# A hybrid decoder layer: low-part score products in 64-row pairs, attention steps of two heads per key head, x chunks in three pieces

## The chip, the cores and the metric

The kernel runs on one core of one Trainium2 chip. The metric is device microseconds of one execution; the figure given for a kernel is the median of several runs. The profile is of one execution of its own, and its times are counted from the start of its span.

## The reference

One layer over 16 learned meta tokens and 1024 tokens of 1024 features, in float32:

```python
u = rmsnorm(h, g_pre_mix)
q, k, v, xr, yr = split(u @ w_in)       # 512, 128, 128, 512, 512 columns
attn = sliding_window_attention_with_sinks(q, k, v, sinks)   # 8 heads of 64, 2 key heads
xr = causal_depthwise_conv(xr, conv_w, conv_b)               # 4 taps
hr = rg_lru(xr, w_a, b_a, w_x, b_x, lru_lambda)              # gates, then a scan over time
h = h + rmsnorm(concat(attn, gelu(yr) * hr) @ w_out, g_post_mix)
h = h + rmsnorm(square(relu(rmsnorm(h) @ w_ff1)) @ w_ff2, g_post_ffn)
```

In the attention a block of 128 queries sees two blocks of 128 keys, its own and the one before, of which the mask leaves a window of 128. Four query heads share one key head: heads 0 to 3 the first, 4 to 7 the second. Each head has a sink, a score without a value.

## The kernel before

Operands of matmuls have the type float32r. Each is split into a high part (a cast to that type on ACT, L96) and a low part (what the cast leaves over, a subtraction on DVE, L99). A product is then three matmuls into one bank of PSUM: high by high, high by low, low by high (`mm3`, L125, L130, L131). Weights are split in this way as they arrive.

The work on the core runs in stages.

- **Opening stage.** The tokens come in four pieces (`ALL`: 272, 256, 256, 256). Of each piece the rows are normed and transposed into `u`, and projected to keys, to values, to the first query pair (`q0`) and to the first x chunk (`xr0`). The first piece is written out by hand with `part` (L282), the others go through `project`, one bank of 24 matmuls per weight and piece. The columns of `u @ w_in` are handled 128 at a time. A query pair j holds heads j and j + 4, one of each key head. The weights of the first x chunk are loaded (L383) ahead of the last four loads of x (L147).
- **Attention stage.** Eight steps: query pair j = 0 to 3, and half = 0, 1 (four query blocks each). `scores(j, half, q)` makes the scores of both heads of the pair for four blocks and turns them into softmax weights; `attend` of the step before transposes the weights (L675), splits them, masks them with selects on POOL (L680) and multiplies them with the values (L691). Between the two, `next_fill` puts one projection of 128 columns on the list: q1, x1, q2, x2, q3, x3, then the four y chunks (the last two of these between the gates). A fill of q or y goes in two pieces of 512 tokens (`REAL2`), one of x in the four of `ALL`, followed by its convolution on DVE (L715, L720).
- **Gates** of the recurrence (L817): 64-row matmuls, two at a time on the two halves of the rows, in pieces of 348, 348 and 344 tokens; then the scan, the output projection, and the two feed-forward products, which fill the rest of the span.

Queries are stored so that one matmul does two of the three products. `q[h]` has the high part of head h in its own 64 rows and the low part in the other 64. `khh[h]` has the high keys in both halves. One matmul of 128 rows (L625) therefore sums high by high and low by high. The second (L629) multiplies `q[h]` with `kl[h]`, which holds the low keys in the head's own rows and zeros in the others:

```python
nc.tensor.matmul(dst, q[h][:, c], hi, start=True, stop=False)    # L625
nc.tensor.matmul(dst, q[h][:, c], lo, start=False, stop=True)    # L629
```

Each matmul has 256 columns, the keys of two blocks. Two blocks of one head share a bank of the tag `s`, of which there are two; ACT copies the scores of the own block out (L642) and DVE those of the block before that the mask keeps (L643). The first query block takes its keys from `km`, where the meta tokens stand.

What an engine does next is set by a planner: it walks through the instructions of the program in the order of their priority, simulates the times, and gives an engine the first instruction whose operands and buffers are ready. Fills are issued with `deferred`, at a lower priority, so they go where attention work waits. Buffers come from groups with a fixed count (`b` 17, `c` 8, `d` 4, `ws` 5, and two banks each of `acc`, `s`, `pt`, `o`).

Of the kernel before, what the change touches and what calls it, by code (L numbers as in the profile page):

```python
# [37 lines left out]
def hybrid_layer(  # L38
# [30 lines left out]
    def f32(ap):  # L69
        return ap.bitcast(F32)  # L70
# [217 lines left out]
    ALL = [(0, 272), (272, 256), (528, 256), (784, 256)]  # L288
    REAL2 = [(16, 512), (528, 512)]

    khh = [slot("b", [P, T], F32R) for _ in range(2)]
    kl = [slot("b", [P, T], F32R) for _ in range(2)]
    HALF = (slice(0, HD), slice(HD, P))
    for h in range(2):
        nc.gpsimd.memset(f32(kl[h][HALF[1 - h]]), 0.0)

# [99 lines left out]
    load_x(3)  # L398
    rx = fetch([(X_COL, P)], "e")
    for i in range(4, 8):  # L400
# [9 lines left out]
    km = slot("ws", [P, 4, 2 * P], F32R)  # L410
    nc.gpsimd.memset(f32(km[:, 0:2, 0 : P - NMETA]), 0.0)
    nc.gpsimd.memset(f32(km[:, 2:4, :]), 0.0)
    nsink = const.tile([P, 8], F32, name="nsink")
# [21 lines left out]
    def low_k(hh, lo, src):  # L435
        return [
            nc.vector.tensor_tensor(
                lo[h][HALF[h]], src[HALF[h]], f32(hh[h][HALF[h]]), op=ALU.subtract
            ).ins
            for h in range(2)  # L440
        ]

    def sink_k(acc, t0, n):
        o = NMETA if t0 == 0 else 0
        c = slice(t0 + o - NMETA, t0 - NMETA + n)
        parts = [([khh[0][:, c], khh[1][:, c]], [kl[0][:, c], kl[1][:, c]], acc[:, o:])]
        if o:

            m, mk = slice(0, NMETA + P), slice(P - NMETA, 2 * P)
            parts.append(  # L450
                ([km[:, 0, mk], km[:, 1, mk]], [km[:, 2, mk], km[:, 3, mk]], acc[:, m])
            )
        ops = [[], []]
        for hh, lo, src in parts:
            ops[0] += high_k(hh, src)
        for hh, lo, src in parts:
            ops[1] += low_k(hh, lo, src)
        if o:
            for e in range(2):
                for ins in ops[e]:  # L460
                    chained(e, ins)
# [34 lines left out]
    q0, sink_q0 = new_q()  # L496
    xr0, sink_x0 = new_x("c")
    for b in range(4):
# [3 lines left out]
        if b == 0:  # L502
# [10 lines left out]
            sink_v(acc[1][:, : piece[1]], *piece)  # L513
            wx = high_w(rx)
            low_w(wx, rx)
            for w, (t0, n), sink, tag in (
                (wq, (16, 256), sink_q0, "o"), (wx, piece, sink_x0, "acc"),
            ):
# [8 lines left out]
        project(wq, [piece], sink_q0)  # L527
        project(wx, [piece], sink_x0)
        done.append(last_mm[0])
# [78 lines left out]

    def scores(j, half, q):

# [4 lines left out]
        for h in range(2):  # L615
            nc.gpsimd.tensor_copy(
                sn[:, h, :, P], nsink[:, j + 4 * h : j + 4 * h + 1].to_broadcast([P, 4])
            )
        for h in range(2):
            for bp in range(2):  # L620
                sp_ = bank("s", (P, 2, 256))

                def qk(dst, b, hi, lo):
                    c = slice(b * P, (b + 1) * P)
                    nc.tensor.matmul(  # L625
                        dst, q[h][:, c], hi, start=True, stop=False,
                        skip_group_check=True,
                    )
                    nc.tensor.matmul(  # L629
                        dst, q[h][:, c], lo, start=False, stop=True,  # L630
                        skip_group_check=True,
                    )

                for i in range(2):
                    b = 4 * half + 2 * bp + i
                    if b == 0:
                        qk(sp_[:, i, :], b, km[:, h, :], km[:, 2 + h, :])
                    else:
                        c = slice((b - 1) * P, (b + 1) * P)
                        qk(sp_[:, i, :], b, khh[h][:, c], kl[h][:, c])  # L640
                s_ = sn[:, h, 2 * bp : 2 * bp + 2, 0:P]
                nc.scalar.copy(s_, sp_[:, :, P:256])  # L642
# [3 lines left out]
                )  # L646
                if half == 0 and bp == 0:
                    w = slice(0, P - NMETA)
                    nc.vector.copy_predicated(
                        sn[:, h, 0, w], above_i[:, w], far.to_broadcast([P, P - NMETA])  # L650
                    )
            nc.vector.tensor_reduce(
                negm[:, h, :], sn[:, h], axis=mybir.AxisListType.X, op=ALU.min
# [12 lines left out]

    def attend(j, half, sn):
        flat = sn.rearrange("p a b c -> p (a b c)")
        pp = []
        for h in range(2):  # L670
# [7 lines left out]
            for p_ in (ph, pl):  # L678
                for s, g, op in ((1, 1, ALU.is_ge), (0, -1, ALU.is_gt)):
# [3 lines left out]
                    )  # L683
            pp.append([t_.rearrange("p a b c -> p (a b c)") for t_ in (ph, pl)])
        for h in range(2):
            po = bank("o")

            def av(kb, oc, n, pc, first, last):
                v = vm[:, h, :] if kb == 0 else vk[h][:, kb - 1, :]
                for k, p_ in enumerate(pp[h]):  # L690
                    nc.tensor.matmul(  # L691
                        po[:, oc : oc + n], v, p_[:, pc : pc + n],
                        start=first and k == 0, stop=last and k == 1,
                        skip_group_check=True,
                    )

            kb0 = 4 * half
            av(kb0, 0, P, 0, True, False)
            for i in range(3):
                av(kb0 + 1 + i, i * P, 256, P + 256 * i, False, False)  # L700
            av(kb0 + 4, 3 * P, P, 7 * P, False, True)

# [3 lines left out]
            nc.vector.tensor_tensor(whole, po[r, :], whole, op=ALU.add)  # L706
        ah, al = at[half][j // 2]
        split(ah[:, j % 2, :], al[:, j % 2, :], flat[:, 0:512])

# [25 lines left out]
    def fill_x(c):  # L735
        def run(w):
            xr, sink = new_x()
            project(w, ALL, sink)
            conv(c, xr, "b" if c == 3 else "d")
        return run  # L740
# [12 lines left out]

    qs = [q0] + [None] * 3
    conv(0, xr0)
    fills = []
    for kind, j in (("q", 1), ("x", 1), ("q", 2), ("x", 2), ("q", 3), ("x", 3)):
        if kind == "q":
# [15 lines left out]
    prev = None  # L774
    for j in range(NPAIR):
        for half in range(2):
            if j % 2 == 0 and half == 0:
                at_pair(j // 2)
            gate_after = last_lut[0]
            sn = scores(j, half, qs[j])  # L780
            if True:
                with deferred(FILL_LAG):
                    next_fill()
            if prev is not None:
                attend(*prev)
            prev = (j, half, sn)
    attend(*prev)


# [14 lines left out]
    def gates(c):  # L804
# [4 lines left out]
        z = [slot("c", [P, TT]) for _ in range(2)]  # L809
        for t0, n in ((0, 348), (348, 348), (696, 344)):  # L810
            acc = []
# [697 lines left out]
```

## Time and profile before

| | |
|---|---|
| timed runs | 961.83, 956.39, 958.47 us, median 958.47 |
| span of the profiled execution | 955.3 us; the profile gives no other time for it |
| mean granted clock of TensorE | 0.998 |
| opening stage, first score product | to about 60 us |
| attention stage | about 60 to 186 us |
| gates | 196.6 to 211 us |
| matmuls in the whole kernel | 4728 |
| score products | 64 at L625, 64 at L629 |
| attention products | 160 at L691 |

The profile's lines give start and duration of an instruction or a group, the engine, the line of the source, the operation, output and input by the program's names (buffer numbers left out), and for a matmul rows and columns of the weights and of the moving operand. PE is TensorE's matmul side, PEld its loading of weights, DVE VectorE, ACT ScalarE, POOL GpSimd, SP SyncE, whose queue issues most DMAs.

### The profile page before, as it was taken

To read this page: it belongs to the slowest core of one execution; us is meant where nothing else is said; L and a number is where in the kernel's file an instruction comes from. 1 tells how busy PE (TensorE), PEld (TensorE's weight loads), DVE (VectorE), ACT (ScalarE), POOL (GpSimd) and SP (SyncE) were. 2 spreads that over 40 slices of the span, in tenths; PEclk is the share of its full clock that TensorE was granted. 3 is DMA by queue.
4 is the path that set the end of the run, shared out by engine and by line. 5 is a ranking of instruction groups with operands and counts; after the bars stand their busy time and mean duration, and the time that the engine had idled before them with its cause. 6 is when DMAs were issued, how large, how long until landed. Compare 5 with 4: busy or idle time off the path is not lost.

```text
span 955.3 us, 12432 instructions
## 1 busy us (share of the span) xinstructions
PE 943.8 (99%) x4728; PEld 789.7 (83%) x4728; DVE 655.7 (69%) x845; ACT 505.9 (53%) x854; POOL 129.1 (14%) x189
## 2 busy tenths in 40 slices
PE   9999999999999999999999999999999999999996
PEld 8999999877888878888888888888887788888885
DVE  6567987788856787665644465476667576779893
ACT  7537766568645554444655575654433343446441
POOL 4102563520021100010000000001121100001201
PEclk9999999999999999999999999999999999999999
DMA  8221010204226368674422364334777765647934
GB/s 271 56 67 23 24 45 24 67 23 131 83 109 185 133 220 264 198 253 144 155 89 88 111 203 127 104 113 114 175 180 186 185 199 177 192 139 196 246 65 89
DMA packets 88199, 130.21 MB, mean 136 GB/s; under 512 B 13702, under 2 KB 52630, under 8 KB 88140
## 3 DMA queue, kind: packets, MB, share of 16 engines
q1 hardware_dynamic: 78972, 104.44, 34.0%
q0 software_dynamic: 8880, 24.19, 12.2%
q8 instruction: 37, 0.61, 0.3%
q10 hardware_dynamic: 288, 0.79, 0.2%
q14 instruction: 22, 0.18, 0.1%
HBM read 109.93 MB, written 18.87 MB: 135 GB/s over the span
## 4 chain that ended last, share of the span: by engine, by line
PE 88%; DVE 5%; ACT 3%; DMA 2%; POOL 1%; issue 1%; SPq 0%; DVEq 0%; ACTq 0%; POOLq 0%
PE ps_acc L130 10%; PE ps_acc L131 10%; PE ps_acc L125 10%; PE ps_s L131 6%; PE ps_s L130 6%; PE ps_s L125 6%; PE ps_pt L130 6%; PE ps_pt L131 6%; PE ps_pt L125 6%; PE ps_o L130 5%; PE ps_o L131 5%; PE ps_o L125 5%; ACT c L82 1%; PE ps_o L691 1%; PE ps_acc L282 1%
## 5 line engine op out<-in xcount | busy, mean ns | idle before, releaser
L99 DVE TENSOR_TENSOR ws<-raw,ws 128x1024 fp32r<-128x1024 f32 (+1 forms) x69 | 82.6, 1197 | 76.1 <-ACT ws L96 24.3
L96 ACT CAST ws<-raw 128x1024 fp32r<-128x1024 f32 (+1 forms) x68 | 69.7, 1026 | 87.9 <-PE ps_o L130 23.9
L96 ACT CAST ws<-e 128x1024 fp32r<-128x1024 f32 x41 | 43.0, 1049 | 82.8 <-PE ps_o L130 35.3
L125 PE MATMUL ps_acc<-a,ws 128*128 128x256 f32 (+2 forms) x256 | 85.8, 335 | 0.0
L130 PE MATMUL ps_acc<-a,ws 128*128 128x256 f32 (+2 forms) x256 | 85.5, 334 | 0.0
L131 PE MATMUL ps_acc<-a,ws 128*128 128x256 f32 (+2 forms) x256 | 85.0, 333 | 0.0
L99 DVE TENSOR_TENSOR b<-b,b 128x1024 fp32r<-128x1024 f32 (+2 forms) x50 | 58.9, 1177 | 24.8 <-PE ps_o L130 19.1
L96 ACT CAST b<-b 128x1024 fp32r<-128x1024 f32 (+2 forms) x49 | 49.9, 1019 | 46.4 <-DVE b L996 41.0
L99 DVE TENSOR_TENSOR ws<-e,ws 128x1024 fp32r<-128x1024 f32 x41 | 50.1, 1223 | 32.4 <-ACT ws L96 18.9
L680 POOL TENSOR_SCALAR_AFFINE_SELECT c<-c 128x512 fp32r<-128x512 f32 x64 | 53.6, 858 | 67.6 <-ACT c L96 59.3
L125 PEld LDWEIGHTS ps_acc<-a,ws 128*128 128x128 f32 x256 | 48.3, 189 | 4.7 <-issue 0.2
L131 PEld LDWEIGHTS ps_acc<-a,ws 128*128 128x128 f32 x256 | 48.3, 189 | 4.5
L130 PEld LDWEIGHTS ps_acc<-a,ws 128*128 128x128 f32 x256 | 48.2, 188 | 4.4 <-issue 0.4
L125 PE MATMUL ps_acc<-ws,b 128*128 128x512 f32 (+1 forms) x120 | 46.3, 387 | 1.1 <-ACT ws L96 1.1
L130 PE MATMUL ps_acc<-ws,b 128*128 128x512 f32 (+1 forms) x120 | 46.3, 386 | 0.5 <-DVE ws L99 0.4
L131 PE MATMUL ps_acc<-ws,b 128*128 128x512 f32 (+1 forms) x120 | 46.1, 385 | 0.0
L125 PE MATMUL ps_pt<-ws,b 128*128 128x512 f32 x112 | 44.4, 396 | 0.0
L130 PE MATMUL ps_pt<-ws,b 128*128 128x512 f32 x112 | 44.1, 394 | 0.0
L131 PE MATMUL ps_pt<-ws,b 128*128 128x512 f32 x112 | 44.0, 393 | 0.0
L125 PE MATMUL ps_s<-ws,b 128*128 128x512 f32 x110 | 43.4, 395 | 0.0
L131 PE MATMUL ps_s<-ws,b 128*128 128x512 f32 x110 | 43.3, 394 | 0.0
L130 PE MATMUL ps_s<-ws,b 128*128 128x512 f32 x110 | 43.3, 393 | 0.0
(416 smaller groups left out, 2662.0 us busy)
## 6 DMA issues: line engine op xcount, KB each, us to landing
raw<-in_w_ff_dram SPq DMA_DIRECT2D x61, 512.0 KB, 4.1
e<-in_w_ff_dram SPq DMA_DIRECT2D x45, 512.0 KB, 4.0
a<-in_w_ff_dram SPq DMA_DIRECT2D x12, 512.0 KB, 6.6
s_dram<-a POOLq DMA_DIRECT2D x12, 512.0 KB, 3.7
c<-in_x_dram SPq DMA_DIRECT2D x8, 512.0 KB, 4.0
raw<-in_w_in_dram SPq DMA_DIRECT2D x8, 512.0 KB, 3.7
d<-in_x_dram SPq DMA_DIRECT2D x8, 512.0 KB, 3.3
out_dram<-raw SPq DMA_DIRECT2D x8, 512.0 KB
```

Source lines behind the costliest of these rows:

```text
L82: ins = nc.scalar.activation(*args, **kwargs).ins
L96: nc.scalar.copy(hi, src)
L99: low = nc.vector.tensor_tensor(lo, src, f32(hi), op=ALU.subtract).ins
L125: ins = nc.tensor.matmul(dst, lh, rh, start=start, stop=False, skip_group_check=True).ins
L130: nc.tensor.matmul(dst, lh, rl, start=False, stop=False, skip_group_check=True)
L131: last_mm[0] = nc.tensor.matmul(dst, ll, rh, start=False, stop=stop, skip_group_check=True).ins.name
L282: last_mm[0] = nc.tensor.matmul(acc[:, :n], w[k // 2][:, kc, :], u[kc][k % 2][:, t0 : t0 + n], start=k == 0 and kc == 0, stop=k == last an ...
L680: nc.gpsimd.affine_select(out=p_[:, :, s], in_=f32(p_[:, :, 0]), pattern=[[0, 4], [g, P]], compare_op=op, fill=0.0, base=0, channel_multip ...
L691: nc.tensor.matmul(po[:, oc : oc + n], v, p_[:, pc : pc + n], start=first and k == 0, stop=last and k == 1, skip_group_check=True,)
```

## The change

- The low keys of both key heads stand in one tile `kl`, each in its own half. Their products take only the head's own 64 rows, of the queries as of the keys. For each query block the order is now: high product of head 0, of head 1 (128 rows), low product of head 0, of head 1 (64 rows), with a bank for each head.
- A step of the attention has two query pairs (so two heads per key head) and two query blocks (a quarter), in place of one pair and four blocks. In `attend`, one matmul covers both heads of a key head, with an operand and an output of two runs of columns: three matmuls for each part of the weights, where there were five.
- The second query pair (`q1`) is projected in the opening stage, where the first x chunk was; the x chunk becomes the first fill. The fills are then x0, q2, x1, q3, x2, x3, and the y chunks as before.
- The x chunks are projected in three pieces of 348, 348 and 344 tokens (`THIRDS`).

```diff
@@ -287,14 +287,13 @@
     ALL = [(0, 272), (272, 256), (528, 256), (784, 256)]
     REAL2 = [(16, 512), (528, 512)]
+    THIRDS = [(0, 348), (348, 348), (696, 344)]
     khh = [slot("b", [P, T], F32R) for _ in range(2)]
-    kl = [slot("b", [P, T], F32R) for _ in range(2)]
+    kl = slot("b", [P, T], F32R)
     HALF = (slice(0, HD), slice(HD, P))
-    for h in range(2):
-        nc.gpsimd.memset(f32(kl[h][HALF[1 - h]]), 0.0)
     zeros = slot("ws", [P, 512], F32R)
@@ -396,7 +395,7 @@
     load_x(2)
     load_x(3)
-    rx = fetch([(X_COL, P)], "e")
+    rq1 = fetch([(Q_COL + HD, HD), (Q_COL + 5 * HD, HD)], "e")
     for i in range(4, 8):
         load_x(i)
@@ -408,8 +407,7 @@
     low_w(wq, rq)
     km = slot("ws", [P, 4, 2 * P], F32R)
-    nc.gpsimd.memset(f32(km[:, 0:2, 0 : P - NMETA]), 0.0)
-    nc.gpsimd.memset(f32(km[:, 2:4, :]), 0.0)
+    nc.gpsimd.memset(f32(km[:, 0:3, 0 : P - NMETA]), 0.0)
     nsink = const.tile([P, 8], F32, name="nsink")
     nc.sync.dma_start(nsink, attn_sinks[0].partition_broadcast(P))
@@ -435,7 +433,7 @@
         return [
             nc.vector.tensor_tensor(
-                lo[h][HALF[h]], src[HALF[h]], f32(hh[h][HALF[h]]), op=ALU.subtract
+                lo[HALF[h]], src[HALF[h]], f32(hh[h][HALF[h]]), op=ALU.subtract
             ).ins
             for h in range(2)
@@ -443,12 +441,12 @@
         o = NMETA if t0 == 0 else 0
         c = slice(t0 + o - NMETA, t0 - NMETA + n)
-        parts = [([khh[0][:, c], khh[1][:, c]], [kl[0][:, c], kl[1][:, c]], acc[:, o:])]
+        parts = [([khh[0][:, c], khh[1][:, c]], kl[:, c], acc[:, o:])]
         if o:
             m, mk = slice(0, NMETA + P), slice(P - NMETA, 2 * P)
             parts.append(
-                ([km[:, 0, mk], km[:, 1, mk]], [km[:, 2, mk], km[:, 3, mk]], acc[:, m])
+                ([km[:, 0, mk], km[:, 1, mk]], km[:, 2, mk], acc[:, m])
             )
         ops = [[], []]
@@ -494,7 +492,7 @@
     done = [None, None]
     q0, sink_q0 = new_q()
-    xr0, sink_x0 = new_x("c")
+    q1, sink_q1 = new_q()
     for b in range(4):
         if b:
@@ -511,10 +509,10 @@
             part(acc[1], wv, piece, 2)
             sink_v(acc[1][:, : piece[1]], *piece)
-            wx = high_w(rx)
-            low_w(wx, rx)
+            wq1 = high_w(rq1)
+            low_w(wq1, rq1)
             for w, (t0, n), sink, tag in (
-                (wq, (16, 256), sink_q0, "o"), (wx, piece, sink_x0, "acc"),
+                (wq, (16, 256), sink_q0, "o"), (wq1, (16, 256), sink_q1, "acc"),
             ):
                 acc = bank(tag)
@@ -525,7 +523,7 @@
         project(wv, [piece], sink_v)
         project(wq, [piece], sink_q0)
-        project(wx, [piece], sink_x0)
+        project(wq1, [piece], sink_q1)
         done.append(last_mm[0])
     for h in range(2):
@@ -606,49 +604,50 @@
-    def scores(j, half, q):
+    def scores(jp, quarter):
         sn = slot("c", [P, 2, 4, P + 1])
...
         rden = small.tile([P, 2, 4], F32, name="rden", tag="rden")
         for h in range(2):
-            nc.gpsimd.tensor_copy(
-                sn[:, h, :, P], nsink[:, j + 4 * h : j + 4 * h + 1].to_broadcast([P, 4])
-            )
-        for h in range(2):
-            for bp in range(2):
-                sp_ = bank("s", (P, 2, 256))
-
-                def qk(dst, b, hi, lo):
-                    c = slice(b * P, (b + 1) * P)
+            for jj in range(2):
+                k = 2 * jp + jj + 4 * h
+                nc.gpsimd.tensor_copy(
+                    sn[:, h, 2 * jj : 2 * jj + 2, P], nsink[:, k : k + 1].to_broadcast([P, 2])
+                )
+        for jj in range(2):
+            q = qs[2 * jp + jj]
+            sps = [bank("s", (P, 2, 256)) for _ in range(2)]
+            for i in range(2):
+                b = 2 * quarter + i
+                cq, ck = slice(b * P, (b + 1) * P), slice((b - 1) * P, (b + 1) * P)
+                for h in range(2):
                     nc.tensor.matmul(
-                        dst, q[h][:, c], hi, start=True, stop=False,
-                        skip_group_check=True,
+                        sps[h][:, i, :], q[h][:, cq],
+                        khh[h][:, ck] if b else km[:, h, :],
+                        start=True, stop=False, skip_group_check=True,
                     )
+                for h in range(2):
+                    r = HALF[h]
                     nc.tensor.matmul(
-                        dst, q[h][:, c], lo, start=False, stop=True,
-                        skip_group_check=True,
+                        sps[h][:, i, :], q[h][r, cq], kl[r, ck] if b else km[r, 2, :],
+                        start=False, stop=True, skip_group_check=True,
                     )
-
-                for i in range(2):
-                    b = 4 * half + 2 * bp + i
-                    if b == 0:
-                        qk(sp_[:, i, :], b, km[:, h, :], km[:, 2 + h, :])
-                    else:
-                        c = slice((b - 1) * P, (b + 1) * P)
-                        qk(sp_[:, i, :], b, khh[h][:, c], kl[h][:, c])
-                s_ = sn[:, h, 2 * bp : 2 * bp + 2, 0:P]
+            for h in range(2):
+                sp_ = sps[h]
+                s_ = sn[:, h, 2 * jj : 2 * jj + 2, 0:P]
                 nc.scalar.copy(s_, sp_[:, :, P:256])
                 nc.vector.copy_predicated(
...
                     sp_[:, :, 0:P],
                 )
-                if half == 0 and bp == 0:
+                if quarter == 0:
                     w = slice(0, P - NMETA)
                     nc.vector.copy_predicated(
-                        sn[:, h, 0, w], above_i[:, w], far.to_broadcast([P, P - NMETA])
+                        sn[:, h, 2 * jj, w], above_i[:, w], far.to_broadcast([P, P - NMETA])
                     )
+        for h in range(2):
             nc.vector.tensor_reduce(
                 negm[:, h, :], sn[:, h], axis=mybir.AxisListType.X, op=ALU.min
@@ -664,7 +663,7 @@
         return sn
-    def attend(j, half, sn):
+    def attend(jp, quarter, sn):
         flat = sn.rearrange("p a b c -> p (a b c)")
         pp = []
@@ -681,31 +680,32 @@
                         compare_op=op, fill=0.0, base=0, channel_multiplier=-g,
                     )
-            pp.append([t_.rearrange("p a b c -> p (a b c)") for t_ in (ph, pl)])
+            pp.append((ph, pl))
+        kb0 = 2 * quarter
         for h in range(2):
             po = bank("o")
-
-            def av(kb, oc, n, pc, first, last):
-                v = vm[:, h, :] if kb == 0 else vk[h][:, kb - 1, :]
+            two = po.rearrange("p (j c) -> p j c", j=2)
+            for n, (oc, pc, w) in enumerate(((0, 0, P), (0, P, 2 * P), (P, 3 * P, P))):
+                kb = kb0 + n
+                v = vk[h][:, kb - 1, :] if kb else vm[:, h, :]
                 for k, p_ in enumerate(pp[h]):
                     nc.tensor.matmul(
-                        po[:, oc : oc + n], v, p_[:, pc : pc + n],
-                        start=first and k == 0, stop=last and k == 1,
+                        two[:, :, oc : oc + w], v,
+                        p_.rearrange("p (j i) s c -> p j (i s c)", j=2)[:, :, pc : pc + w],
+                        start=n == 0 and k == 0, stop=n == 2 and k == 1,
                         skip_group_check=True,
                     )
-
-            kb0 = 4 * half
-            av(kb0, 0, P, 0, True, False)
-            for i in range(3):
-                av(kb0 + 1 + i, i * P, 256, P + 256 * i, False, False)
-            av(kb0 + 4, 3 * P, P, 7 * P, False, True)
             r, o = HALF[h], HALF[1 - h]
...
             nc.scalar.copy(whole, po[o, :])
             nc.vector.tensor_tensor(whole, po[r, :], whole, op=ALU.add)
-        ah, al = at[half][j // 2]
-        split(ah[:, j % 2, :], al[:, j % 2, :], flat[:, 0:512])
+        ah, al = at[quarter // 2][jp]
+        c = slice(256 * (quarter % 2), 256 * (quarter % 2) + 256)
+        split(
+            ah[:, :, c], al[:, :, c],
+            flat[:, 0:512].rearrange("p (j c) -> p j c", j=2),
+        )
@@ -735,7 +735,7 @@
         def run(w):
             xr, sink = new_x()
-            project(w, ALL, sink)
+            project(w, THIRDS, sink)
             conv(c, xr, "b" if c == 3 else "d")
         return run
@@ -751,10 +751,9 @@
         return run
-    qs = [q0] + [None] * 3
-    conv(0, xr0)
+    qs = [q0, q1, None, None]
     fills = []
-    for kind, j in (("q", 1), ("x", 1), ("q", 2), ("x", 2), ("q", 3), ("x", 3)):
+    for kind, j in (("x", 0), ("q", 2), ("x", 1), ("q", 3), ("x", 2), ("x", 3)):
         if kind == "q":
             fills.append((lambda j=j: w_q(j), fill_q(j)))
@@ -772,18 +771,16 @@
     prev = None
-    for j in range(NPAIR):
-        for half in range(2):
-            if j % 2 == 0 and half == 0:
-                at_pair(j // 2)
+    for jp in range(2):
+        at_pair(jp)
+        for quarter in range(4):
             gate_after = last_lut[0]
-            sn = scores(j, half, qs[j])
-            if True:
-                with deferred(FILL_LAG):
-                    next_fill()
+            sn = scores(jp, quarter)
+            with deferred(FILL_LAG):
+                next_fill()
             if prev is not None:
                 attend(*prev)
-            prev = (j, half, sn)
+            prev = (jp, quarter, sn)
     attend(*prev)
@@ -807,7 +804,7 @@
         z = [slot("c", [P, TT]) for _ in range(2)]
-        for t0, n in ((0, 348), (348, 348), (696, 344)):
+        for t0, n in THIRDS:
             acc = []
             for s in range(2):
```

## The prediction

> **What bounds the kernel now.** I read the page first: busy shares, then the chain that ended last; then the busy time by stretches of 20 us; then the PE timeline of the attention stage, matmul by matmul.
>
> ```profile
> PE 943.8 (99%) x4728; PEld 789.7 (83%) x4728; DVE 655.7 (69%) x845; ACT 505.9 (53%) x854; POOL 129.1 (14%) x189
> ...
> PE 88%; DVE 5%; ACT 3%; DMA 2%; POOL 1%; issue 1%; SPq 0%; DVEq 0%; ACTq 0%; POOLq 0%
> ```
>
> PE is busy for 99% of the 955.3 us and carries 88% of the chain. But busy PE is not PE at its peak, so the stage that the change touches (scores, softmax and attention products, with projections as filling work between them) has to be looked at by itself. The columns are: stretch, its length, then busy time and count of instructions of PE, PEld, DVE, ACT and POOL, the granted clock, DMA share and GB/s.
>
> ```profile
> 20.00:40.00 20.00, 20.00 (x170) 19.64 (x169) 13.77 (x30) 12.06 (x30) 5.11 (x13) 1.00 0.31 81
> ...
> 100.00:120.00 20.00, 20.00 (x134) 18.24 (x133) 19.45 (x31) 13.31 (x42) 12.06 (x13) 1.00 0.09 28
> 120.00:140.00 20.00, 20.00 (x156) 19.21 (x155) 17.54 (x30) 13.77 (x45) 12.25 (x18) 1.00 0.15 43
> 140.00:160.00 20.00, 19.68 (x138) 18.25 (x137) 16.39 (x28) 12.75 (x37) 8.48 (x13) 1.00 0.13 38
> ```
>
> PE has nearly no idle time in the stage, although DVE is close behind it (19.45 of 20). Filling projections cover every softmax. So here the sum of PE's issue intervals sets the end: each interval removed or added on PE moves it by as much, and time saved on ACT, DVE or POOL moves nothing. The duration of a matmul (about 280 ns at 256 columns) is not its price, because matmuls overlap; the price is the step from one start to the next:
>
> ```profile
> 73.99 0.28 PE L625 MATMUL ps_s<-ws,b 128*128 128x256 f32 x1
> ...
> 74.81 0.28 PE L629 MATMUL ps_s<-b,b 128*128 128x256 f32 x1
> ```
>
> These are the first and the last of a group of eight score products: seven intervals take 0.82 us, 0.117 each, which I use for 256 columns.
>
> **The change part by part.** First the low parts of the scores.
>
> ```profile
> L625 PE MATMUL ps_s<-b,b x56: 275/281/366, 65.8 to 165.8; 128*128 128x256 f32 x56
> ...
> L625 PE MATMUL ps_s<-ws,b x8: 278/282/367, 59.7 to 155.1; 128*128 128x256 f32 x8
> ```
> ```profile
> L629 PE MATMUL ps_s<-b,b x56: 275/280/288, 66.0 to 165.9; 128*128 128x256 f32 x56
> ...
> L629 PE MATMUL ps_s<-ws,b x8: 279/281/282, 59.9 to 155.2; 128*128 128x256 f32 x8
> ```
>
> There are 64 high products (L625) and 64 low ones (L629). The high ones stay. The 64 low ones become 64-row products of the two heads, rows 0 to 63 and 64 to 127, in separate banks, so as 32 pairs. The gates (L817) already run such pairs, and show both what a pair costs and what it costs to get in and out of 64-row work:
>
> ```profile
> 196.29 0.40 PE L125 MATMUL ps_acc<-a,ws 128*128 128x512 f32 x1
> 196.62 0.43 PE L817 MATMUL ps_s<-b,e 64*128 64x348 f32 x1
> 196.62 0.43 PE L817 MATMUL ps_pt<-b,e 64*128 64x348 f32 x1
> 196.89 0.32 PE L817 MATMUL ps_o<-b,e 64*128 64x348 f32 x1
> 196.89 0.32 PE L817 MATMUL ps_s<-b,e 64*128 64x348 f32 x1
> ...
> 198.00 0.32 PE L817 MATMUL ps_pt<-b,e 64*128 64x344 f32 x1
> 198.00 0.32 PE L817 MATMUL ps_o<-b,e 64*128 64x344 f32 x1
> 198.25 0.51 PE L130 MATMUL ps_acc<-a,ws 128*128 128x512 f32 x1
> 198.59 0.40 PE L131 MATMUL ps_acc<-a,ws 128*128 128x512 f32 x1
> ...
> 200.21 0.40 PE L125 MATMUL ps_acc<-a,ws 128*128 128x512 f32 x1
> ```
>
> The two of a pair start together, so a pair costs one interval: seven intervals from 196.89 to 198.00, 0.159 each at 348 columns. A 512-column matmul costs 0.231 (seven intervals from 198.59 to 200.21). Pairing therefore saves half the low products: 32 x 0.117 = 3.8 us.
>
> Now the switch. From the start at 196.29 to that at 198.59 are 2.30 us. They hold two 512-column intervals (0.46) and nine pairs (9 x 0.159 = 1.43), 1.89 in all. So 0.41 us are spent on going in and out. The first matmul on either side also shows a longer time (0.43 against 0.32, 0.51 against 0.40), as if it waited until the pipe had emptied: a 512-column matmul that lasts 0.40 and frees its place after 0.231 leaves 0.17 to wait, and the switch is 0.2 each way. The next gate block repeats it to the hundredth, which a wait for data would not:
>
> ```profile
> 201.59 0.40 PE L125 MATMUL ps_acc<-a,ws 128*128 128x512 f32 x1
> ...
> 203.89 0.40 PE L131 MATMUL ps_acc<-a,ws 128*128 128x512 f32 x1
> ```
>
> The new loop issues, for each query block: high, high, low pair. So it goes into 64-row work and out again 32 times (2 key steps x 4 quarters x 2 heads x 2 blocks): 32 x 0.41 = 13.1 us. A 256-column matmul leaves the same to wait as a 512-column one (0.28 - 0.117 = 0.16), so I see no reason for less. What the gates don't show is a short run. The nearest row is the transposes of 8 rows between transposes of 128:
>
> ```profile
> 22.15 0.38 PE L357 MATMUL ps_pt<-ident,d 128*128 128x128 f32 x2
> 22.37 0.38 PE L357 MATMUL ps_s<-ident,d 128*128 128x128 f32 x2
> ```
> ```profile
> 52.60 0.38 PE L357 MATMUL ps_s<-ident,d 128*128 128x128 f32 x2
> 52.91 0.41 PE L539 MATMUL ps_o<-ident,d 8*128 8x8 f32 x4
> 53.26 0.44 PE L598 MATMUL ps_pt<-ident,c 128*128 128x128 f32 x2
> ```
> ```profile
> L539 PE MATMUL ps_o<-ident,d 8*128 8x8 f32 x4 | 0.4, 207 | 0.0
> ```
>
> By their ends (52.98, 53.32, 53.70) the four small ones add 0.34 and the two after them 0.38. Undisturbed, two transposes take 0.22 (22.15 to 22.37) and the four (0.41 - 0.207)/3 x 4 = 0.27. That is 0.07 in and 0.16 out, 0.23 together. So a run of four pays too. I keep 0.23 and 0.41 as the ends (7.4 and 13.1 us) and take 0.41, because its rows have the same 64-row form. That it falls on each switch however short the run is also what the Trainium skill says, on the page TensorEngine Tiling (Array Packing), section Key Properties: changing the tiling mode drains the engine; no row here shows a run of a single pair.
>
> Next, fewer and wider matmuls. Two of 256 columns cost 0.235, one of 512 costs 0.231: a matmul merged away saves 0.004 us. Attention products go from 160 to 96 with the same columns:
>
> ```profile
> L691 PE MATMUL ps_o<-c,b x144: 219/279/337, 89.2 to 185.3; 128*128 128x256 f32 x96, 128*128 128x128 f32 x48
> ...
> L691 PE MATMUL ps_o<-c,e x16: 221/223/327, 87.7 to 172.9; 128*128 128x128 f32 x16
> ```
>
> 64 x 0.004 = 0.3 us saved. Four x chunks in three pieces save 4 x 24 matmuls; the second query pair, which moves into the opening stage and there goes in four pieces instead of two, adds 48. Net 48 x 0.004 = 0.2 us saved. Both are bounded by zero and half a microsecond; the operand in two runs of columns that the wide attention products read has no row here, and I give it no price of its own.
>
> Work off PE: in the opening stage, the second query pair takes the place of the first x chunk, piece by piece.
>
> ```profile
> 24.84 0.86 DVE L479 SCALAR_TENSOR_TENSOR b<-ps_o,b 64x256 fp32r<-64x256 f32 x2
> ```
> ```profile
> 21.70 0.77 ACT L476 ACTIVATE b<-ps_o 64x256 fp32r<-64x256 f32 x2 [0.55 <-PE ps_o L282]
> ...
> 26.09 0.39 ACT L490 COPY c<-ps_acc 128x272 f32<-128x272 f32 x1 [1.67 <-PE ps_acc L282]
> ```
>
> Each of four pieces swaps one ACT copy (0.39) for two (0.77) and adds 0.86 on DVE: 1.5 and 3.4 us in all. DVE has 6 us free in 20 to 40 and PE runs on the next piece's transposes, so I cost it at nothing; uncovered it would be up to 3.4 us, through the two banks of the tag acc that stay taken longer. On SP's queue the load of the x chunk (0.44 us of issue) becomes two issues ahead of the last four x loads:
>
> ```profile
> 10.36 0.44 SPq L383 DMA_DIRECT2D e<-in_w_in_dram  x1
> ```
>
> They slip by another 0.44 us at most; hidden, since their first users are the later transposes, behind projections that fill PE. On POOL the sink copies go from two to four a step:
>
> ```profile
> L616 POOL COPY c<-nsink 128x4 f32<-128x4 f32 x12 | 3.3, 308 | 0.0
> ```
>
> Sixteen more at up to 0.308 are 4.9 us, spread over a stage in which POOL is idle for 8 us of every 20; the selects queued behind a copy would start 0.6 us later per step, and PE has fill work for that. The two memsets that go are at the start, off the chain.
>
> One more term comes from the order in which score banks come free. In a group of eight, the two banks are now one of each head. If the second is still being read, the low product of the first head goes alone. The groups of before are sometimes cut in that way:
>
> ```profile
> 110.27 0.28 PE L629 MATMUL ps_s<-b,b 128*128 128x256 f32 x1
> 111.89 0.28 PE L625 MATMUL ps_s<-b,b 128*128 128x256 f32 x1
> ```
>
> Here a group of eight breaks after four. Cut like this, a group goes through four round trips instead of two and has four low intervals instead of two: 2 x 0.41 + 2 x 0.117 = 1.1 us. I count one such group of the sixteen, at 1.1.
>
> Sum: -3.8 (pairs) -0.3 -0.2 (merged) +13.1 (switches) +1.1 (one cut group) = +9.9 us on PE, none of it covered, as PE has no idle time in the stage and carries the chain after it. The profiled execution would go from 955.3 to 965.2; the timed runs' median is 958.47, 3.2 above that span, and I carry this difference over: 958.47 + 9.9 = 968.4 us.
>
> **The rivals.** *The switch hides in short runs.* Then the time falls by 4.3 us, to 954.2. It decides below 4.3/32 = 0.13 us per round trip. For it: no row shows one pair alone. Against it: the 8-row run paid 0.23, the gate blocks 0.41 each. The Trainium skill, page TensorE: Matmul & The Clock Gate, section Measured speedup vs the span model, prices a pack at a matmul plus about 4 ns a tile and has no term for a switch; by it the sum would be about -4.2, and the gate rows differ with 0.41 us. Chance 0.12.
>
> *Half the groups are cut or more.* Eight cut groups add 8 x 1.1 in place of 1.1, sixteen 17.6: 976 to 985 us. For it, each head's bank now feeds a separate copy; against it, most groups of before run whole. Chance 0.08.
>
> *Buffers starve PE near the end of the stage.* The convolution of the last x chunk and two y chunks need buffers that the last query pairs hold until the last scores. If PE lacks filling work there, it waits for the softmax. One fill is 48 x 0.231 = 11.1 us; half of it without cover gives 5.5 more, 973 us (less without the cut group). Against it: the two acc banks let one y chunk run ahead, and the order of before has the same kind of wait. Chance 0.08.
>
> *The pairs don't run together,* so the change doesn't do what it says: 3.8 us are not saved, 972 us. The gates speak against it. Chance 0.05.
>
> **How the numbers follow.** The forecast keeps 0.67, with its own range 961 (0.23 per round trip, no cut group: +7.4 - 4.3 = 3.1) to 973 (0.41 and five cut groups: +13.1 - 4.3 + 5.5 = 14.3). Leaving out the hidden switch (0.12) below and the many cuts (0.08) above, 961 to 975 holds 0.80. A measurement of this kernel can tell about 0.5%, 4.8 us, from no change. The hidden switch lies at that bound: half of it faster, half the same. Of the forecast, 0.04 falls within the bound. So faster 0.06, same 0.10, slower 0.63 + 0.08 + 0.08 + 0.05 = 0.84.
>
> **What would show it.** In the PE timeline after, starts in a score group should run: high, 0.12, high, about 0.2 to 0.3, low pair together, about 0.2 to 0.3, high; about 0.76 to 0.78 us per query block where it was 0.47. The weight loads should sit idle at each such place. 112 matmuls fewer should stand in the page, and the stage should end about 10 us later with PE still without idle. Wrong would be: blocks of 0.36 us (no switch), the two low ones 0.12 apart, or idle PE before attention products.

## The result and the profile after

The changed kernel takes 973.51 us (median of four runs, 972.78 to 975.84) against 958.0 for the kernel before: 15.5 us slower, a ratio of 1.0172 with a 95% interval of 1.0151 to 1.0194. (The ratios here and below are those on record, taken over the runs; they are not the quotients of the medians, which here would be 1.0162.) The forecast was 968.4, range 961 to 975. Sign and cause were right; the size was a third too small, and three parts of the sum (the low products, the attention products, the gates) were wrong in ways that partly cancel. The profiled run took 975.84 us, of which the span is 973.9.

The page of the changed kernel, busy shares and the chain by engine:

```profile
PE 960.4 (99%) x4616; PEld 791.1 (81%) x4616; DVE 657.4 (67%) x849; ACT 507.2 (52%) x854; POOL 121.1 (12%) x202
...
PE 89%; DVE 4%; DMA 3%; ACT 2%; issue 1%; SPq 0%; DVEq 0%; ACTq 0%
```

112 matmuls fewer, as forecast, and PE is busy for 16.6 us longer. Two stretches of the attention stage (the columns are as in the prediction):

```profile
80.00:100.00 20.00, 20.00 (x99) 15.81 (x100) 15.65 (x26) 12.45 (x43) 7.37 (x12) 1.00 0.09 27
120.00:140.00 20.00, 20.00 (x97) 15.78 (x96) 17.45 (x26) 12.59 (x32) 9.91 (x20) 1.00 0.09 27
```

PE is still busy throughout. Some 98 matmuls are counted in each stretch, against 134 to 156 in the full stretches of the stage shown of before, and the loading of weights has fallen to 15.8 us of 20. The counts alone prove little: in both stretches projections of 512 columns fall (52 of the matmuls), and the other three stretches between 100 and 180 us have 112 to 121. What counts is that PE waits for no engine in the stage; its own steps have become longer. The score products by source line, the high ones first (count, shortest/median/longest in ns, first and last start):

```profile
L626 PE MATMUL ps_s<-b,b x56: 275/362/392, 66.3 to 186.5; 128*128 128x256 f32 x56
```
```profile
L633 PE MATMUL ps_s<-b,b x56: 379/381/391, 66.7 to 186.7; 64*128 64x256 f32 x56
```

Every low product (L633) shows about 380 ns where 280 was usual, and most high ones have become longer as well: the mark by which the prediction read a switch in the gates. One group of eight in the order of time, between two projections:

```profile
102.31 0.32 PE L130 MATMUL ps_acc<-a,ws 128*128 128x348 f32 x1
102.46 0.28 PE L626 MATMUL ps_s<-b,b 128*128 128x256 f32 x1
102.67 0.38 PE L633 MATMUL ps_s<-b,b 64*128 64x256 f32 x1
102.98 0.51 PE L626 MATMUL ps_s<-b,b 128*128 128x256 f32 x2
103.41 0.38 PE L633 MATMUL ps_s<-b,b 64*128 64x256 f32 x1
103.73 0.38 PE L626 MATMUL ps_s<-b,b 128*128 128x256 f32 x1
104.04 0.39 PE L633 MATMUL ps_s<-b,b 64*128 64x256 f32 x2
104.36 0.43 PE L131 MATMUL ps_acc<-a,ws 128*128 128x348 f32 x1
104.63 0.33 PE L125 MATMUL ps_acc<-a,ws 128*128 128x348 f32 x1
```

The order of the source would be high, high, low pair, high, high, low pair: two runs of 64-row work. Here it is high, low, high, high, low, high, low pair: three runs, two of them single. The place on PE is the same for both kinds: from the single low at 103.41 to the next matmul 0.32 us, from the pair at 104.04 to the next 0.32 us. So a pair does run as one, and a low product that has lost its partner costs as much as a pair. Over the stage I count 48 runs, 32 of one product and 16 of a pair. Of the sixteen groups 2 are whole, 12 are cut in one block and 2 in both. The weight loads at the first switch of the same stretch stand idle where the prediction said:

```profile
102.67 0.18 PEld L633 LDWEIGHTS ps_s<-b,b 64*128 64x128 f32 x1 [0.17 <-issue]
```

### The profile page after: what moved, and what is told of

It reads as the page before. It is cut to its first block, busy times and chain, and to the rows that moved or that the text cites. A ratio compares the mean times of both kernels' runs of the same rounds, so it can differ in the third digit from the quotient of the medians.

```text
span 973.9 us, 12224 instructions
## 1 busy us (share of the span) xinstructions
PE 960.4 (99%) x4616; PEld 791.1 (81%) x4616; DVE 657.4 (67%) x849; ACT 507.2 (52%) x854; POOL 121.1 (12%) x202
## 4 chain that ended last, share of the span: by engine, by line
PE 89%; DVE 4%; DMA 3%; ACT 2%; issue 1%; SPq 0%; DVEq 0%; ACTq 0%
PE ps_acc L125 11%; PE ps_acc L131 10%; PE ps_acc L130 10%; PE ps_s L125 6%; PE ps_s L131 6%; PE ps_s L130 6%; PE ps_pt L131 6%; PE ps_pt L125 6%; PE ps_pt L130 6%; PE ps_o L125 5%; PE ps_o L130 5%; PE ps_o L131 5%; PE ps_o L692 2%; PE ps_s L633 2%; PE ps_s L626 1%
## 5 line engine op out<-in xcount | busy, mean ns | idle before, releaser
L125 PE MATMUL ps_acc<-a,ws 128*128 128x512 f32 (+3 forms) x240 | 83.9, 350 | 0.0
L131 PE MATMUL ps_acc<-a,ws 128*128 128x512 f32 (+3 forms) x240 | 83.2, 347 | 0.0
L130 PE MATMUL ps_acc<-a,ws 128*128 128x512 f32 (+3 forms) x240 | 82.5, 344 | 0.0
L679 POOL TENSOR_SCALAR_AFFINE_SELECT c<-c 128x512 fp32r<-128x512 f32 x64 | 48.3, 780 | 98.8 <-ACT c L96 95.9
L125 PEld LDWEIGHTS ps_acc<-a,ws 128*128 128x128 f32 x240 | 45.2, 188 | 5.1 <-issue 1.1
L131 PEld LDWEIGHTS ps_acc<-a,ws 128*128 128x128 f32 x240 | 45.1, 188 | 4.9 <-issue 0.7
L130 PEld LDWEIGHTS ps_acc<-a,ws 128*128 128x128 f32 x240 | 45.1, 188 | 3.8 <-issue 0.2
```

What stands on the lines that cost most here:

```text
L125: ins = nc.tensor.matmul(dst, lh, rh, start=start, stop=False, skip_group_check=True).ins
L130: nc.tensor.matmul(dst, lh, rl, start=False, stop=False, skip_group_check=True)
L131: last_mm[0] = nc.tensor.matmul(dst, ll, rh, start=False, stop=stop, skip_group_check=True).ins.name
L679: nc.gpsimd.affine_select(out=p_[:, :, s], in_=f32(p_[:, :, 0]), pattern=[[0, 4], [g, P]], compare_op=op, fill=0.0, base=0, channel_multip ...
```

## The experiments

Each kernel was timed beside the kernel before on the same chip; I compare ratios. "Planner" is the program that sets the order of the instructions. The theory: every run of 64-row products costs a round trip on PE, whatever its length, and the rest of the change is small. The rivals: the rest of the change costs the part that the forecast missed; or a 64-row product is slow by itself, in whatever order.

**Without 64 rows.** In the changed kernel:

```diff
-  r = HALF[h]
...
-  sps[h][:, i, :], q[h][r, cq], kl[r, ck] if b else km[r, 2, :],
+  sps[h][:, i, :], q[h][:, cq], kl[:, ck] if b else km[:, 2, :],
```

> The changed kernel with its low products over all 128 rows of the one tile of low keys (the low queries of a head then also meet the low keys of the other head, a term of the size of low by low), so that no matmul of the stage has 64 rows; order, steps, fills and pieces as changed. Switch theory (each run of 64-row products costs a round trip of 0.39 us on PE, the changed kernel has 48 such runs, of which 32 are single products): 973.5 - 48 x 0.39 + 16 x 0.117 = 956.7 us, 0.5 below the kernel before within what can be told. Rival 'rest of the change' (the 5.6 us beyond the forecast come from the new steps, the late x chunk or buffers that are held longer): 963 to 964 us. Rival 'narrow products' (a 64-row product is slow by itself, about 0.25 us more each, in whatever order): 957.5 us, so this run does not part it from the first.

Measured: 955.21 us against 954.27, ratio 1.0004 (0.9995 to 1.0013). All the loss goes with the 64-row form. As ratios the switch theory had 0.9986 (956.7 against 958.0) and the rival "rest of the change" 1.005 or more; the interval holds neither, but the theory is off by 0.002 and the rival by 0.005. The rest of the change, taken together, does nothing that can be told, and that rival falls.

**Lows by four, and pairs kept.** Both chain the products of a group with the ordering edges that the kernel has already (`behind`):

```diff
+  for low in range(2):          # by four: this loop outside, then i, then h
+      for i in range(2):        # pairs kept: i outside, then low, then h
...
+                  if prods:
+                      behind(prods[-1], ins)
```

> The changed kernel with the eight products of a pair of banks put in a fixed order: four high ones, then the four low ones of 64 rows, so 16 runs of two pairs. Switch theory: 973.5 - 32 x 0.39 - 16 x 0.117 = 959.1 us. Rival 'rest of the change': about 966 us (963.6 + 16 x 0.39 - 32 x 0.117). Rival 'narrow products': no change, 973.5 us.

> The changed kernel with the order of its source made fixed: high, high, low, low for each query block, so 32 runs, each of one pair, as the prediction had it. Switch theory: 973.5 - 16 x 0.39 - 16 x 0.117 = 965.4 us. Rival 'rest of the change' (cut groups cost nothing): 973.5 us. Rival 'narrow products': 973.5 us, or 1.9 less if pairs overlap.

Measured: by four 960.98 us, ratio 1.0068 (1.0054 to 1.0082); pairs kept 966.48 us, ratio 1.0123 (1.0107 to 1.0138). The order alone, with the same products, moves the time from 1.0179 (the changed kernel again, below) to 1.0123 and 1.0068. So the rival "narrow products" falls. Both still come out above what the switch theory expected (959.1 and 965.4 against 958.0, ratios of 1.0011 and 1.0077). In part this is because the edges don't forbid other work in between, so the runs are 20 and 34 and not 16 and 32, and in part because those times start from 973.5, a quotient of 1.0162, where the changed kernel stands at 1.0179 here. More on it below. (The scores by four lack the high products of the first block of each bank; that kernel is read for its time alone.)

**The kernel before with lone 64-row lows.**

```diff
+  r = HALF[h]
...
-  dst, q[h][:, c], lo, start=False, stop=True,
+  dst, q[h][r, c], lo[r], start=False, stop=True,
```

> The kernel before with one edit: its low products take only the 64 rows of their head, in the old order high, low, high, low of one head, so 64 runs of a single product and no pair. Switch theory: 958.0 + 64 x 0.39 = 983.0 us. Rival 'rest of the change' says the same here. Rival 'narrow products': 958.0 + 64 x 0.25 = 974 us. If 64 rows were cheaper by themselves: below 958.

Measured: 978.66 us against 954.27, ratio 1.0253 (1.0239 to 1.0267), 24.4 us for 64 runs, 0.38 each (expected were 25 by the switch theory and 16 by the rival "narrow products"). One edit in the kernel before, with its own steps and fills, costs more than the whole change. A group of it in time:

```profile
97.20 0.39 PE L630 MATMUL ps_s<-ws,b 64*128 64x256 f32 x1
97.52 0.38 PE L625 MATMUL ps_s<-b,b 128*128 128x256 f32 x1
97.83 0.38 PE L630 MATMUL ps_s<-b,b 64*128 64x256 f32 x1
98.14 0.39 PE L625 MATMUL ps_s<-b,b 128*128 128x256 f32 x1
98.46 0.38 PE L630 MATMUL ps_s<-b,b 64*128 64x256 f32 x1
```

From low to low are 0.63 us, for two intervals of 0.117: 0.39 us for in and out together. Half of it falls on each side (0.31 or 0.32 from each start to the next). The Trainium skill's rule that a change of tiling mode drains the engine (TensorEngine Tiling (Array Packing), Key Properties) agrees with the trace here for a run of one product, at 0.39 us a round trip, which is what no row of before could show.

**The changed kernel again, gates held together, narrow attention products, lows by eight.** After the first four runs the sum still needed about -3 us from somewhere, and the profile of the changed kernel showed the gates in pieces:

```profile
208.12 0.42 PE L814 MATMUL ps_s<-b,e 64*128 64x348 f32 x1
...
208.63 0.50 PE L125 MATMUL ps_acc<-a,ws 128*128 128x512 f32 x1
208.97 0.40 PE L130 MATMUL ps_acc<-a,ws 128*128 128x512 f32 x1
209.29 0.42 PE L814 MATMUL ps_s<-b,e 64*128 64x348 f32 x1
```

Before, each of four chunks ran its 18 products in one piece. Now projections and the last attention products come between, in ten runs instead of four.

> The changed kernel itself, to have it beside the others on one chip: ratio 1.017. The sum as it now stands: 48 runs of low products, 32 of one (0.508 us) and 16 of a pair (0.513 us), 24.5 us, for 64 x 0.1175 = 7.5 us before: +16.9; gates in ten runs for four: +2.4; what is left, about -3, would have to be the wider attention products and x pieces, for which the prediction had -0.5.

Measured: 972.57 us, ratio 1.0179 (1.0166 to 1.0193).

The gates in full_rows, chained, with the first of a chunk behind the last reader of the banks:

```diff
-  nc.tensor.matmul(
+  ins = nc.tensor.matmul(
...
+  behind(held[0], ins)
+  held[0] = ins.name
...
+  held[0] = read              # the chunk's last sigmoid
```

> The kernel full_rows (new steps, low products over 128 rows) with the gate products put in a fixed order, each chunk's first one held behind the last reader of the banks, so that the planner lays them out in five runs of 64-row work, where full_rows has ten and the kernel before four. Theory (a run of gates costs its round trip of 0.41 us too, and the new steps had broken the gates up): 5 x 0.41 = 2.1 us less than full_rows, a ratio of 0.998 to the kernel before, below 1 beyond its interval. Rival (the broken gates fill places in which PE would wait anyway): no change, 1.000.

Measured: 958.11 us against 955.79, ratio 1.0029 (1.0015 to 1.0044): slower than full_rows (1.0004), against the theory. The waits of PE between 190 and 270 us (engine and line that waited, whom for, us in total, times, longest), for this kernel:

```profile
PE ps_pt L125 <- ACT b L96: 3.3, 1, 3.3
PE ps_s L815 <- ACT c L82: 1.0, 1, 1.0
```

The five runs are there, but PE waits 1.0 us inside one of them and 3.3 us later, at the output projection, for a split. full_rows waits 1.7 us there in all, so the waits take back what five runs fewer would save (5 x 0.39 = 2.0 us) and 0.6 us more; why the kernel is slower by 2.4 us (by the ratios) isn't shown. As I read it, the broken gates fill places in which PE would wait, and their round trips can't simply be taken out.

Each wide attention product as two, in full_rows:

```diff
-  two[:, :, oc : oc + w], v,
+  two[:, j, oc : oc + w], v,          # for j in range(2)
```

> The kernel full_rows with each wide attention product as two, one for each query pair: 192 attention products for 96, the columns of all the same. The prediction's price (0.004 us for each matmul merged away): +0.4 us, a ratio of 1.001 to the kernel before, not to be told from full_rows. Rival (the remainder of about -3 us comes from the 64 products merged away, 0.04 to 0.05 each): +4 us, 1.005.

Measured: 961.11 us, ratio 1.0060 (1.0048 to 1.0072), 5.4 us above full_rows: the rival's figure and more. The trace says why a narrow product is not cheap. First a 128-column attention product among projections in the kernel before, then two of them in narrow_av:

```profile
87.56 0.28 PE L125 MATMUL ps_acc<-a,ws 128*128 128x256 f32 x1
87.68 0.22 PE L691 MATMUL ps_o<-c,e 128*128 128x128 f32 x1
87.74 0.34 PE L130 MATMUL ps_acc<-a,ws 128*128 128x256 f32 x1
87.91 0.28 PE L131 MATMUL ps_acc<-a,ws 128*128 128x256 f32 x1
```
```profile
90.37 0.33 PE L692 MATMUL ps_o<-c,e 128*128 128x128 f32 x2
```

The start after the 128-column product comes 0.06 us later, but that matmul is 0.06 longer and the one behind it starts 0.17 after it: the two take 0.23 where 0.06 + 0.117 would be 0.18. Two of 128 columns together take 0.33 where one takes 0.22, so the second adds 0.11. So a 128-column product with new weights costs about 0.11 us here, nearly the price of one of 256 columns. It is no floor for every matmul: the four 8-row transposes in the prediction, with weights of 8 rows, add 0.07 each. The Trainium skill (TensorE: Matmul & The Clock Gate, LDWEIGHTS (loading the stationary operand)) gives the load of 128 columns as 128/1.2 = 107 ns. The 0.111 agrees with that, and so does the step between two loads that the trace of before has beside the first of these lines (87.68 and 87.79), though the record of each load lasts 0.19. That the load is what sets the price is not shown: no run here changes the width of the weights.

At 0.111 each, the products of a key head in a step go from 2 x (2 x 0.117 + 0.231) = 0.93 to 2 x (4 x 0.111 + 2 x 0.117) = 1.36 us, and sixteen of these add 6.8 us. Against that, the gates lie in 8 runs here for the 10 of full_rows (0.8 us), and PE doesn't wait at the output projection, where full_rows waits 1.7 us; with both the sum is 4.3. The measured 5.4 lies between.

Four banks to a step, all eight highs and then all eight lows:

```diff
+  prods, banks = [], [[bank(tag, (P, 2, 256)) for _ in range(2)] for tag in ("s", "pt")]
```

> The changed kernel with four banks to a step (two of the tag s, two of pt) and a fixed order: the step's eight high products, then its eight low ones of 64 rows in four pairs, so eight or nine runs. Switch theory: a run of n pairs costs 0.39 + n x 0.117 us, here 0.86; eight of them 6.9 us for 7.5 before, so the low products come out even and the kernel at full_rows, ratio 0.999 to 1.000. Rival 'narrow products': as slow as the changed kernel, 1.017. Rival (banks of pt held by scores keep the transposes of the softmax weights waiting): PE stands idle in the stage and the ratio is 1.003 or more.

Measured: 960.08 us, ratio 1.0037 (1.0022 to 1.0051). There are 13 runs and not 8, because the longest are cut too. By the price of a run (0.39 us, and 0.117 for each pair or single product in it: 13 x 0.39 + 36 x 0.117 = 9.3 us) that is 1.8 us over the 7.5 of whole rows; measured are 3.2 over full_rows. The time is that of the last rival (1.003 or more), but its sign is missing: PE has no idle time in the stage. It waits 2.8 us around the gates and the output projection, where full_rows waits 1.7. The gates lie in 5 runs here for 10 there, which should save up to 2.0 us. So of 1.4 to 3.4 us over the sum the waits explain 1.1, and the rest is not settled.

**Two attempts at a faster version**, both on full_rows:

```diff
-  (("x", 0), ("q", 2), ("x", 1), ("q", 3), ("x", 2), ("x", 3))
+  (("x", 0), ("x", 1), ("q", 2), ("q", 3), ("x", 2), ("x", 3))   # x_first
...
+  next_fill()                 # y_before_gates: ahead of the gates
   for c in range(NLRU):
       gates(c)
...
-  next_fill()
```

> An attempt at a version that beats both: the kernel full_rows with the fills of the stage in the order x0, x1, q2, q3, x2, x3. The planner then lays the gates out in eight runs for full_rows' ten. By the round trip alone 2 x 0.41 = 0.8 us less than full_rows: ratio 0.9995 to the kernel before. If it goes as in the run with the gates held (fewer runs bought with waits of PE): 1.000 to 1.003. A gain that can be told from the kernel before needs 0.998 or less: only if PE waits less ahead of the output projection as well.

> The other attempt: full_rows with the third y chunk put on the list ahead of the gates, so that PE has a projection more while the last attention steps leave their banks. Eight runs of gates for ten: 0.8 us less than full_rows, 0.9995; if the waits ahead of the output projection (1.7 us longer in full_rows than in the kernel before) go as well, 0.998; if the y chunk only delays the gates and the recurrence behind them, 1.002 or more.

Measured: x_first 955.81 us, ratio 1.0009 (1.0000 to 1.0018), no gain. y_before_gates 965.87 us, ratio 1.0119 (1.0105 to 1.0133): 11 us lost, in waits of PE at the output projection between 195 and 290 us:

```profile
PE ps_pt L125 <- ACT b L96: 8.5, 2, 6.1
PE ps_pt L125 <- ACT a L96: 1.8, 1, 1.8
```

As I read it, the projection moved ahead of the gates had covered the recurrence behind them. No kernel here beats the one before.

## Why the prediction was right in sign and short in size

Point by point, with the records of the changed kernel:

- **The bound was right.** PE's intervals set the end of the stage; taking the switches away gave back all of the loss (full_rows).
- **The price of a round trip was right.** 0.41 us taken from the gates, 0.39 measured for runs of one product; the low end, 0.23 from the 8-row transposes, was too low. The rival "the switch hides in short runs" is refuted.
- **The number of round trips was the step that failed.** The sum had 32 of them and one cut group at 1.1 us. There are 48. I read the whole groups of eight in the trace of before as a sign that the new ones would stay whole. But there the second bank is touched only after four products (0.47 us) on the first; now it is needed after one (0.12 us). That the order makes the difference is shown (pairs_kept: 34 runs, ratio 1.0123 for 1.0179); why the planner broke it is not. The reason that the prediction gave for a cut group, a second bank that is still being read, does not show on the chip. The last reads of both banks before the group at 102.46 are these, on ACT and DVE:

```profile
97.73 0.65 ACT L640 COPY c<-ps_s 128x256 f32<-128x256 f32 x2
98.34 0.76 DVE L641 COPY_PREDICATED c<-above,ps_s 128x256 f32<-128x256 int32 x2
```

They end at 99.10, 3.4 us ahead, and in every group but the stage's first both banks were read out at least 2.7 us ahead. If the bank was the reason, it was so only in the times that the planner simulated. The rival "half the groups are cut or more", at 0.08, is what happened, at a smaller price: mostly one block of two is cut, 0.39 + 0.117 = 0.51 us, not 1.1.

- **The pairs run together,** as said, but only 16 were left: 16 x 0.117 = 1.9 us saved for 3.8.
- **The merged attention products were mis-sized.** At 0.004 us each the term was -0.3. With 0.111 for a 128-column product, a head's products in a step go from 2 x (2 x 0.111 + 3 x 0.117) = 1.15 to 2 x (2 x 0.117 + 0.231) = 0.93 us, and sixteen of these save 3.5 us.
- **The gates were missing from the sum.** Six more round trips cost 6 x 0.39 = 2.3 us. In three of the ten runs products have also lost their partners, which makes 41 intervals of 36, 5 x 0.159 = 0.8 us. And PE waits in the output projection, first before (between 190 and 270 us), then after (between 200 and 285), 1.1 us more:

```profile
PE ps_pt L130 <- DVE a L99: 0.2, 1, 0.2
```
```profile
PE ps_pt L131 <- DVE b L99: 1.3, 3, 0.8
```

The sum as it should have been: 48 x 0.39 = 18.7, less 1.9, less 3.5, less 0.2 for the pieces, plus 2.3, plus 0.8, plus 1.1 = +17.3 us, against 15.5 by the medians, 16.5 by the ratio and 17.1 by the ratio of the second timing. With full_rows the same terms without the lows give +0.5, against +0.4 measured (-0.5 to +1.2). That the time fell inside the range was in part luck: the low products were 6.4 us above their part of the sum and the gates 4.2, and only the attention products, at 3.2 below, brought it back under 975.

The kernels with a forced order come out 1.6 and 1.7 us above such sums (by four +4.5 and 6.1 over full_rows, pairs kept +9.7 and 11.4). Part of it lies in the gates: in both traces PE waits there for ACT, which it doesn't in full_rows,

```profile
PE ps_o L817 <- ACT c L82: 0.6, 1, 0.6
```

and the gates have 44 and 46 intervals for 41, another 0.5 and 0.8 us. The rest I have not settled. The starving of PE by late buffers, a rival at 0.08, did not show: PE has no idle time in the stage.

## What to carry to other kernels

A half-height product is not priced by its own time but by the switches around it: count the runs as the order on the engine will have them, not as the source has them, and gather enough of them in one run (here, more than three pairs, as 0.39 us are 3.3 intervals of 0.117) before expecting a gain; that gain is worked out, and no run here shows it. Don't take it from an old order of the planner that a new one will stay whole: here 14 of 16 groups were cut. And price a narrow matmul by the step to the one after the next: the first interval between starts can be short because the following matmul pays (0.06 and then 0.17 us here).

## What was not expected of the hardware

- A 64-row pair costs what a 64-row single costs when 128-row work follows (0.31 to 0.32 us from its start to the next matmul's), so losing the partner is pure loss.
- The round trip has nearly no dependence on the length of the run: 0.41 us with nine pairs, 0.39 with one product.
- A 128-column matmul with weights of its own takes 0.11 us of PE, nearly as much as a 256-column one (0.117), although the start after it comes after 0.06.
